# Projections of a hybrid streaming encoder: the low halves of nine weights and nine mixed inputs move from VectorE to GpSimd

## The chip, the cores and the metric

The kernel runs on one core of a Trainium2 chip. The core has five engines with a queue each: TensorE (PE in the profile; its weight loads are PEld), VectorE (DVE), ScalarE (ACT), GpSimd (POOL) and SyncE (SP, which issues the DMAs). Each works through its own instructions in the order in which they were written out when the program was built, and waits on semaphores where an instruction needs the result of another engine. The metric is the device time of one execution, in microseconds (us); lower is better.

## The reference

Two encoder layers on a sequence of 512 frames with 1024 channels. Layer 0 mixes time with RWKV-7, layer 1 with a Conformer convolution; each is followed by cross-attention to 256 memory tokens and a conv-gated MLP. All inputs and weights are float32. What the change touches is the start of the RWKV mixer, cut to its core here:

```python
xx = jnp.pad(h, ((0, 0), (1, 0), (0, 0)))[:, :T] - h
xr, xw, xk, xv, xa, xg = (h + xx * mu[i] for i in range(6))
r = xr @ w_r                       # 512 x 1024 times 1024 x 1024
k = xk @ w_k
v = xv @ w_v
logw = -softplus(-(w0 + tanh(xw @ w1) @ w2)) - 0.5
decay = exp(-exp(logw))
a = sigmoid(a0 + (xa @ a1) @ a2)
kk = normalised per head(k * k_k)
k = k * (1.0 + (a - 1.0) * k_a)
# then the recurrence over the frames
#   S = S * dec + (S @ -kk) (kk * a)^T + v k^T,   y = S r
# per head of 64 channels, group norm, a bonus from r, k, v, a gate, and @ w_o
```

## The kernel before

Activations lie transposed, 128 channels by 512 frames a tile, eight tiles for 1024 channels. A float32 product is made from three products in a faster format (fp32r): every operand is split into a high half, its cast to fp32r, and a low half, the operand minus that cast, and `mm3` adds high*high, high*low and low*high in PSUM (L181 to L183). The function `split` (L175) does the two steps: ScalarE makes the high half (L176), VectorE the low half by a subtraction with two inputs in SBUF (L177). Every large product of the kernel goes through it.

The three projections run in the order `w_k`, `w_r`, `w_v`. For each, `mixes` makes eight mixed inputs: ScalarE scales h (L368), VectorE adds the shifted part (L369), then `split` gives the pair `xh`, `xl` of 128x512. The input `mf` has two buffers. The weight is read in eight column blocks of 128x1024. The first two blocks are fetched together in two halves by `lead`, so that PE can work on them while the mixed inputs still arrive; the other six (j = 2 to 7) are loaded by SP, split by `wsplit` and used one at a time, 24 matmuls each. The halves `wh` and `wl` have two buffers each: a block's cast can start when PE has finished the block before the previous one.

Other work is woven into the projections. After each block of `w_k`, `k_done` turns k into the decayed keys: matmuls for decay and rate (L521, L540, L541), a long chain on ScalarE and VectorE, and a small weight tile `ws` (ACT L533 and L537, DVE L538) whose zero half GpSimd clears (L532). `r_done` has one product on VectorE with PSUM (L578), two in SBUF (L582) and a matmul (L585). Memory keys and values for the later cross-attention fill gaps (L987, L1043, plain float32). In two groups of four head pairs the kernel inverts small triangular matrices: `subst_a` multiplies (L609), masks (L612), transposes (L618) and then solves by 30 pairs of VectorE steps whose operands all lie in SBUF (L630, L632); `subst_b` transposes the result twice (L640, L642), has GpSimd clear a part of `tt` (L647), copies the rest with ScalarE (L648, L649), and multiplies again (L656, L666). Group 0 starts during `w_k` and ends during `w_r`, group 1 starts during `w_r` and ends during `w_v`. Both lie across the stretches in which the inputs of `w_r` and `w_v` are mixed and split.

Which instruction stands where in an engine's queue is decided by the tile framework's scheduler when the program is built, from the order of the code and its own estimate of durations.

Of the kernel before, what the change touches and what calls it, by code (L numbers as in the profile page):

```python
# [11 lines left out]
ALU = mybir.AluOpType  # L12
# [19 lines left out]
FO = [1, 1, 1, 1, 1, 1, 1, 1]  # L32
FP = 1
NRAW = 4
NGRP = [4, 4, 4, 4, 4, 4, 4, 7]
TB = 'h'
TAS = 'hhhhhhhg'
# [73 lines left out]
class Builder:  # L111
# [51 lines left out]
    def wraw(self, src, cols, rows=128):  # L163
        raw = self.t(self.wp, [128, 1024], "raw", bufs=NRAW)
        self.nc.sync.dma_start(raw[:rows, :cols], src)
        return raw

    def wsplit(self, src, cols):
        raw = self.wraw(src, cols)
        h = self.t(self.wp, [128, 1024], "wh", F32R, bufs=2)  # L170
        l = self.t(self.wp, [128, 1024], "wl", F32R, bufs=2)
        self.split(raw[:, :cols], h[:, :cols], l[:, :cols])
        return h, l

    def split(self, src, h, l):  # L175
        self.nc.scalar.copy(h, src)  # L176
        self.nc.vector.tensor_tensor(out=l, in0=src, in1=h, op=ALU.subtract)  # L177

    def mm3(self, out, lh, ll, rh, rl, start, stop):
        mm = self.nc.tensor.matmul  # L180
# [10 lines left out]
    def lead(self, srcs):  # L191
# [3 lines left out]
        for half in range(2):  # L195
            raw = self.t(self.wp, [128, 1024], "raw", bufs=NRAW)
            for j in range(2):
# [4 lines left out]
            ws.append((h, l))  # L202
        return ws

    def gemm_cols(self, srcs, xs, evac, lead=None, between=None):

        ws = lead or self.lead(srcs)
        pss = [self.ps() for _ in range(2)]
        for k, (xh, xl) in enumerate(xs):
            for j in range(2):  # L210
                w = ws[k // 4]
                s = slice(j * 512 + k % 4 * 128, j * 512 + k % 4 * 128 + 128)
                self.mm3(pss[j], w[0][:, s], w[1][:, s], xh, xl, k == 0, k == len(xs) - 1)
        if between:
            between()
        for j in range(len(srcs)):
            if j < 2:
                ps = pss[j]
            else:
                w = self.wsplit(srcs[j], 1024)  # L220
                ps = self.ps()
                self.gemm(ps, w, xs)
            evac(j, ps)
# [100 lines left out]
    def rwkv(self):  # L324
        nc, a = self.nc, self.a
        with ExitStack() as cx:
# [27 lines left out]
            h = self.x  # L354
# [7 lines left out]
            for i in range(KT):  # L362
                nc.vector.scalar_tensor_tensor(out=h[:, i, :], in0=h[:, i, :], scalar=self.vec("g_mix0", i),
                                               in1=rs, op0=ALU.mult, op1=ALU.mult)

            def mix(m, i, tag="mf", bufs=2):
                mf = self.t(self.gp, [128, T], tag, bufs=bufs)
                nc.scalar.activation(mf, h[:, i, :], AF.Copy, scale=cpr[:, (5 + m) * KT + i : (5 + m) * KT + i + 1])  # L368
                nc.vector.scalar_tensor_tensor(out=mf[:, 1:], in0=h[:, i, : T - 1], scalar=self.vec(f"mu{m}", i),  # L369
                                               in1=mf[:, 1:], op0=ALU.mult, op1=ALU.add)  # L370
                return mf
# [19 lines left out]
            for i in range(KT):  # L391
                mf = mix(5, i, "xh", KT)
# [9 lines left out]
            def mixes(m):  # L402
                xs = []
                for i in range(KT):
                    mf = mix(m, i)
                    xt = self.xtile()
                    self.split(mf, *xt)
                    xs.append(xt)
                return xs

# [4 lines left out]

            rslot = lambda: self.t(self.wp, [128, D], "raw", bufs=NRAW)
            for j in range(NU0, NST):
# [34 lines left out]
            for w, m, done in (("w_k", 2, k_done), ("w_r", 0, r_done),  # L452
                               ("w_v", 3, v_done)):
                srcs = [a[w][p] for p in range(NP)]
                lead = self.lead(srcs)
                self.gemm_cols(srcs, mixes(m), done, lead)
            self.gates = [self.t(r1, [128, T], n) for n in ("za", "zl")]
            nc.sync.dma_start(self.gates[0], self.gpark[0:128])
            for r0 in (0, 32, 64):
# [12 lines left out]
            lead = self.lead(wo)  # L472
# [579 lines left out]
    def xattn(self, layer):  # L1052
        nc, a = self.nc, self.a
        kd, vd = self.kvd[0, layer], self.kvd[1, layer]
        with ExitStack() as cx:
# [67 lines left out]
            for n4 in range(2):  # L1123
                raw = self.t(self.wp, [128, 1024], "raw", bufs=NRAW)
                for j in range(2):
# [13 lines left out]
    def ffn(self, layer):  # L1139
        nc, a = self.nc, self.a  # L1140
        with ExitStack() as cx:
# [63 lines left out]
            if layer == 0:  # L1205
# [3 lines left out]
                for u in self.vunits[:NKV]:  # L1209
                    self.lower(NKP, lambda: u(lambda: self.t(self.wp, [128, D], "raw", bufs=NRAW), lambda: self.t(ap, [128, T], "z", bufs=2)))  # L1210
                del self.vunits[:NKV]


    def conv(self):
        nc, a = self.nc, self.a
        PADW = CW - 1
        with ExitStack() as cx:
# [31 lines left out]
            def in_done(j, ps):  # L1249
# [17 lines left out]
                for h in range(2):  # L1267
                    own, oth = slice(64 * h, 64 * h + 64), slice(64 - 64 * h, 128 - 64 * h)
                    for d, s in zip(s_[h], (uh, ul)):
                        nc.scalar.copy(d[own], s[own])  # L1270
                        nc.scalar.copy(d[oth, 0 : W - 1], s[own, 1:W])  # L1271
                ng = NGRP[i]
                pcs = [self.ps(TP), self.ps(TB)]
# [51 lines left out]
            def late_values():  # L1325
                self.vmem[:] = self.memory1(lambda: self.t(up, [128, D], "kvm", bufs=2))
                for u in self.vunits:
                    u(lambda: self.t(self.wp, [128, D], "raw", bufs=NRAW), lambda: self.t(up, [128, T], "vl", bufs=KT))

# [157 lines left out]
```

## Time and profile before

| what | us |
|---|---|
| median of three runs | 1658.86 |
| the three runs | 1658.69, 1660.44, 1658.86 |
| the profiled execution | 1656.06 |
| its span, first to last instruction | 1654.3 |
| PE busy (share of the span) | 1613.1 (98%) |
| DVE busy | 1106.0 (67%) |
| ACT busy | 794.8 (48%) |
| POOL busy | 73.1 (4%) |

All times of the trace are counted from the start of the span of this one execution. A busy PE is not PE at its peak, because the ends of matmuls are modelled; a wait of PE is what counts. The projections run from about 64 us to about 291 us of the span: `w_k` to 141, `w_r` to 238, `w_v` after that.

### The profile page before, as it was taken

The numbers are of one execution on the slowest core, as the hardware profiler recorded it, in microseconds if no ns is written. First come the engines' busy times: TensorE is split into PE (matmuls) and PEld (weight loads), VectorE is DVE, ScalarE is ACT, GpSimd is POOL, SyncE is SP. The second block draws the span as 40 slices with busy tenths as digits, with TensorE's granted clock in tenths as the row PEclk, the third lists the DMA queues.
The fourth block names the chain that finished last, engine by engine and source line by source line (L and its number), as shares of the span: only waits on it lengthen the run. The fifth ranks groups of instructions, "written<-read, shape, count | busy, mean of one in ns | idle before, by whom it ended". The sixth has DMA issues, their size and how long they took to land. (4 is left out here: it accounts for less than half of the span.)

```text
span 1654.3 us, 24232 instructions
## 1 busy us (share of the span) xinstructions
PE 1613.1 (98%) x9742; PEld 1293.5 (78%) x9742; DVE 1106.0 (67%) x1795; ACT 794.8 (48%) x1242; POOL 73.1 (4%) x101
## 2 busy tenths in 40 slices
PE   7999989899999999999999999999999999999998
PEld 6575558898888888888888777767888888888887
DVE  4779976568766667777732479877766677777323
ACT  5876635766454344434422366645533434444222
POOL 0000000000000000000000024430000000000000
PEclk9999999999999999999999999999999999999999
DMA  6333322103441233332333331223412333323332
GB/s 237 114 99 109 105 65 90 53 22 115 135 140 51 86 120 94 98 103 90 96 95 94 112 107 51 65 89 103 140 52 89 91 98 94 102 92 93 97 95 83
DMA packets 55151, 159.77 MB, mean 97 GB/s; under 512 B 6144, under 2 KB 10368, under 8 KB 55040
## 3 DMA queue, kind: packets, MB, share of 16 engines
q1 hardware_dynamic: 55040, 158.24, 30.8%
q8 instruction: 76, 1.25, 0.3%
q14 instruction: 35, 0.29, 0.1%
HBM read 150.55 MB, written 7.67 MB: 96 GB/s over the span
## 5 line engine op out<-in xcount | busy, mean ns | idle before, releaser
L176 ACT CAST wh<-raw 128x1024 fp32r<-128x1024 f32 (+1 forms) x227 | 235.1, 1037 | 503.4 <-PE g L182 396.2
L182 PE MATMUL g<-xl,wh 128*128 128x512 f32 x1152 | 451.0, 392 | 4.1 <-DVE xl L177 3.6
L181 PE MATMUL g<-xh,wh 128*128 128x512 f32 x1152 | 452.9, 394 | 0.7 <-ACT xh L176 0.7
L183 PE MATMUL g<-xh,wl 128*128 128x512 f32 x1152 | 451.0, 391 | 2.5 <-DVE wl L177 2.5
L177 DVE TENSOR_TENSOR wl<-raw,wh 128x1024 fp32r<-128x1024 f32 (+1 forms) x227 | 274.7, 1210 | 164.2 <-ACT wh L176 163.8
L182 PEld LDWEIGHTS g<-xl,wh 128*128 128x128 f32 x1152 | 216.9, 188 | 54.0 <-DVE xl L177 6.6
L183 PEld LDWEIGHTS g<-xh,wl 128*128 128x128 f32 x1152 | 216.9, 188 | 50.4 <-DVE wl L177 3.3
L181 PEld LDWEIGHTS g<-xh,wh 128*128 128x128 f32 x1152 | 216.9, 188 | 48.4 <-issue 1.8
L181 PE MATMUL g<-ah,wh 128*128 128x512 f32 (+1 forms) x374 | 141.0, 377 | 0.0
L183 PE MATMUL g<-ah,wl 128*128 128x512 f32 (+1 forms) x374 | 140.9, 377 | 0.0
L182 PE MATMUL g<-al,wh 128*128 128x512 f32 (+1 forms) x374 | 140.9, 377 | 0.0
L1157 DVE TENSOR_TENSOR z<-g,rs 128x512 f32<-128x512 f32 x88 | 60.4, 688 | 70.8 <-PE g L183 69.2
L181 PEld LDWEIGHTS g<-ah,wh 128*128 128x128 f32 x374 | 70.4, 188 | 13.0
L182 PEld LDWEIGHTS g<-al,wh 128*128 128x128 f32 x374 | 70.4, 188 | 12.9
L183 PEld LDWEIGHTS g<-ah,wl 128*128 128x128 f32 x374 | 70.4, 188 | 12.7
L1277 POOL TENSOR_TENSOR dg<-i,wsp 128x256 fp32r<-128x256 f32 x70 | 48.2, 721 | 657.3 <-DVE wsp L1231 573.0
L176 ACT CAST ah<-tmp 128x512 fp32r<-128x512 f32 x44 | 27.3, 622 | 100.9 <-DVE z L1156 95.8
L1299 DVE SCALAR_TENSOR_TENSOR h<-u,cdw,h 128x512 f32<-128x512 f32 x98 | 73.8, 753 | 2.3
L321 DVE TENSOR_TENSOR x<-x,g 128x512 f32<-128x512 f32 x39 | 26.8, 688 | 68.7 <-PE g L183 68.7
L1162 DVE SCALAR_TENSOR_TENSOR tmp<-z,fdw,tmp 128x512 f32<-128x512 f32 x88 | 66.0, 752 | 2.9
L1161 DVE SCALAR_TENSOR_TENSOR tmp<-z,fdw,tmp 128x512 f32<-128x512 f32 x88 | 65.5, 746 | 0.4 <-ACT tmp L1160 0.4
L1160 ACT ACTIVATE tmp<-z,fdw 128x512 f32<-128x512 f32 x88 | 63.2, 720 | 4.7 <-DVE z L1157 1.5
(351 smaller groups left out, 2445.4 us busy)
## 6 DMA issues: line engine op xcount, KB each, us to landing
raw<-wi SPq DMA_DIRECT2D x84, 512.0 KB, 3.5
raw<-wo SPq DMA_DIRECT2D x33, 512.0 KB, 3.5
raw<-wv SPq DMA_DIRECT2D x16, 512.0 KB, 3.6
raw<-cwi SPq DMA_DIRECT2D x14, 512.0 KB, 3.6
raw<-wq SPq DMA_DIRECT2D x12, 512.0 KB, 4.4
raw<-wxo SPq DMA_DIRECT2D x12, 512.0 KB, 3.5
raw<-wo SPq DMA_DIRECT2D x16, 384.0 KB, 3.1
raw<-wk SPq DMA_DIRECT2D x10, 512.0 KB, 3.8
```

What stands on the lines that cost most here:

```text
L176: self.nc.scalar.copy(h, src)
L177: self.nc.vector.tensor_tensor(out=l, in0=src, in1=h, op=ALU.subtract)
L181: mm(out, lh, rh, start=start, stop=False)
L182: mm(out, lh, rl, start=False, stop=False)
L183: mm(out, ll, rh, start=False, stop=stop)
L321: self.nc.vector.tensor_tensor(out=self.x[:, n, :], in0=self.x[:, n, :], in1=ps, op=ALU.add)
L1157: nc.vector.tensor_tensor(out=z[:, 2:], in0=ps, in1=rs(), op=ALU.mult)
L1160: nc.scalar.activation(y, z[:, 2:], AF.Copy, scale=cw(2))
L1161: nc.vector.scalar_tensor_tensor(out=y, in0=z[:, 1 : T + 1], scalar=cw(1), in1=y, op0=ALU.mult, op1=ALU.add)
L1162: nc.vector.scalar_tensor_tensor(out=y, in0=z[:, 0:T], scalar=cw(0), in1=y, op0=ALU.mult, op1=ALU.add)
L1277: nc.gpsimd.tensor_tensor(out=dg[:, h], in0=i2.unsqueeze(1).unsqueeze(1).to_broadcast([128, 2, 2, 64]), in1=wsp[:, :, i, h, 2 * g : 2 * g ...
L1299: nc.vector.scalar_tensor_tensor(out=ac, in0=u[:, jt : jt + T], scalar=cw(jt), in1=ac if n else ln["c"], op0=ALU.mult, op1=ALU.add if n el ...
```

## The change

`split` and `wsplit` take an engine for the subtraction, `gemm_cols` takes the set of column blocks whose low half goes to GpSimd. The three projections use it for the blocks j = 3, 5 and 7 of each weight and for the mixed inputs i = 2, 4 and 6. That is nine subtractions of 128x1024 and nine of 128x512. The casts stay on ScalarE, and all other products of the kernel keep VectorE.

```diff
+SPW = (3, 5, 7)
+SPX = (2, 4, 6)
...
-    def wsplit(self, src, cols):
+    def wsplit(self, src, cols, eng=None):
         raw = self.wraw(src, cols)
         h = self.t(self.wp, [128, 1024], "wh", F32R, bufs=2)
         l = self.t(self.wp, [128, 1024], "wl", F32R, bufs=2)
-        self.split(raw[:, :cols], h[:, :cols], l[:, :cols])
+        self.split(raw[:, :cols], h[:, :cols], l[:, :cols], eng)
         return h, l
 
-    def split(self, src, h, l):
+    def split(self, src, h, l, eng=None):
         self.nc.scalar.copy(h, src)
-        self.nc.vector.tensor_tensor(out=l, in0=src, in1=h, op=ALU.subtract)
+        (eng or self.nc.vector).tensor_tensor(out=l, in0=src, in1=h, op=ALU.subtract)
...
-    def gemm_cols(self, srcs, xs, evac, lead=None, between=None):
+    def gemm_cols(self, srcs, xs, evac, lead=None, between=None, other=()):
...
-                w = self.wsplit(srcs[j], 1024)
+                w = self.wsplit(srcs[j], 1024, self.nc.gpsimd if j in other else None)
...
-                    self.split(mf, *xt)
+                    self.split(mf, *xt, nc.gpsimd if i in SPX else None)
...
-                self.gemm_cols(srcs, mixes(m), done, lead)
+                self.gemm_cols(srcs, mixes(m), done, lead, other=SPW)
```

The line numbers of the changed kernel are two higher than before from `split` on (L179 there is L177 here). The order of instructions moves at many places, because the scheduler reckons with the new engine. Three of them follow.

GpSimd, from the second half of `w_k` to the end of `w_v`. Before, it only clears tiles there (`tmp` is `ws`):

```order
L532 MEMSET tmp_1268 128x256
L532 MEMSET tmp_1350 128x256
L647 MEMSET tt_85 32x32x32 x2
L492 MEMSET c_434_2641 64x1024
L492 MEMSET c_435_2642 64x1024
```

In the changed kernel the same queue holds the subtractions (`xl_1464` is input 6 of `w_r`; `wl_1675`, `wl_2044` and `wl_2116` are blocks 3, 5 and 7 of `w_r`; the last six belong to `w_v`):

```order
L534 MEMSET tmp_1268 128x256
L179 TENSOR_TENSOR xl_1464<-mf_1460,xh_1463 128x512
L534 MEMSET tmp_1350 128x256
L179 TENSOR_TENSOR wl_1675<-raw_1672,wh_1674 128x1024
L179 TENSOR_TENSOR wl_2044<-raw_2041,wh_2043 128x1024
L649 MEMSET tt_85 32x32x32 x2
L179 TENSOR_TENSOR wl_2116<-raw_2113,wh_2115 128x1024
L179 TENSOR_TENSOR xl_2185<-mf_2181,xh_2184 128x512
L179 TENSOR_TENSOR xl_2199<-mf_2195,xh_2198 128x512
L179 TENSOR_TENSOR xl_2213<-mf_2209,xh_2212 128x512
L179 TENSOR_TENSOR wl_2310<-raw_2307,wh_2309 128x1024
L179 TENSOR_TENSOR wl_2374<-raw_2371,wh_2373 128x1024
```

Subtractions and memsets now stand behind each other, so each waits until the ones ahead of it have their inputs.

PE, in `w_r`, around the decay matmuls of the last key block (`h_258_1355`; `g_323_1678` is block 3 of `w_r`, `g_330_1784` block 4, `wl_322_1675` the low half that moves to GpSimd). Before:

```order
L182 MATMUL g_323_1678<-xl_278_1422,wh_321_1674 128x512
L1043 MATMUL kv_306_1535<-raw_332_1814,tt_16_85 128x512
L181 MATMUL g_330_1784<-xh_277_1421,wh_328_1780 128x512
L182 MATMUL g_330_1784<-xl_278_1422,wh_328_1780 128x512
L1043 MATMUL kv_306_1535<-raw_332_1814,tt_16_85 128x512
L540 MATMUL h_258_1355<-zw_13_82,tmp_257_1350 128x512
```

In the changed kernel:

```order
L184 MATMUL g_323_1678<-xl_278_1422,wh_321_1674 128x512
L185 MATMUL g_323_1678<-xh_277_1421,wl_322_1675 128x512
L183 MATMUL g_323_1678<-xh_280_1428,wh_321_1674 128x512
L184 MATMUL g_323_1678<-xl_281_1429,wh_321_1674 128x512
L185 MATMUL g_323_1678<-xh_280_1428,wl_322_1675 128x512
L183 MATMUL g_323_1678<-xh_283_1435,wh_321_1674 128x512
L184 MATMUL g_323_1678<-xl_284_1436,wh_321_1674 128x512
L185 MATMUL g_323_1678<-xh_283_1435,wl_322_1675 128x512
L183 MATMUL g_323_1678<-xh_286_1442,wh_321_1674 128x512
L542 MATMUL h_258_1355<-zw_13_82,tmp_257_1350 128x512
```

Eight more matmuls of block 3 stand ahead of the decay matmuls; the two matmuls of block 4 and three matmuls of the memory values (L1043) went behind them.

ScalarE, in `w_v`, at the end of the second substitution (`wh_405_2373` is the high half of block 5 of `w_v`, `wh_412_2416` of block 6, `x_4_60` holds v, `tt_16_85` and `c4_409_2405` belong to the substitution). Before:

```order
L176 CAST wh_405_2373<-raw_404_2371 128x1024
L449 COPY x_4_60<-g_399_2313 128x512
L648 COPY tt_16_85<-c4_409_2405 32x32x32
L649 COPY tt_16_85<-c4_409_2405 32x32x32
L648 COPY tt_16_85<-c4_409_2405 32x32x32
L649 COPY tt_16_85<-c4_409_2405 32x32x32
L176 CAST wh_412_2416<-raw_411_2414 128x1024
```

In the changed kernel:

```order
L650 COPY tt_16_85<-c4_409_2405 32x32x32
L178 CAST wh_405_2373<-raw_404_2371 128x1024
L451 COPY x_4_60<-g_399_2313 128x512
L651 COPY tt_16_85<-c4_409_2405 32x32x32
L650 COPY tt_16_85<-c4_409_2405 32x32x32
L651 COPY tt_16_85<-c4_409_2405 32x32x32
L178 CAST wh_412_2416<-raw_411_2414 128x1024
```

The cast of block 5 now stands behind the first of the four copies, which needs VectorE's last transpose (L642).

## Rows read from the trace of the kernel before

**Rows 1.** Busy us of the engines by stretch of the projections (PE, PEld, DVE, ACT, POOL):
```profile
64.00:125.00 61.00, 59.76 (x454) 48.26 (x454) 43.31 (x83) 44.91 (x79) 3.16 (x6) 1.00 0.35 110
125.00:200.00 75.00, 69.63 (x417) 43.29 (x416) 73.38 (x164) 48.42 (x78) 2.83 (x5) 0.95 0.38 117
219.00:272.00 53.00, 48.22 (x199) 35.85 (x200) 49.82 (x98) 21.59 (x31) 0.95 (x1) 1.00 0.21 62
272.00:295.00 23.00, 23.00 (x376) 19.44 (x376) 6.20 (x6) 17.24 (x24) 0.95 (x1) 1.00 0.47 142
```
**Rows 2.** Waits of PE from 64 to 296 us: total, times, longest:
```profile
PE g L182 <- DVE xl L177: 3.6, 3, 2.6
...
PE h L540 <- DVE tmp L538: 0.2, 1, 0.2
```
**Rows 3.** Timeline, block 3 of `w_r`: start, us, instruction [idle before <-releaser]:
```profile
175.49 1.05 ACT L176 CAST wh<-raw 128x1024 fp32r<-128x1024 f32 x1
...
191.51 1.22 DVE L177 TENSOR_TENSOR wl<-raw,wh 128x1024 fp32r<-128x1024 f32 x1
...
192.78 0.79 PE L183 MATMUL g<-xh,wl 128*128 128x512 f32 x1 [2.48 <-DVE wl L177]
193.37 0.63 PE L181 MATMUL g<-xh,wh 128*128 128x512 f32 x1
193.79 0.63 PE L182 MATMUL g<-xl,wh 128*128 128x512 f32 x1
...
197.40 0.39 PE L182 MATMUL g<-xl,wh 128*128 128x512 f32 x1
197.63 0.39 PE L183 MATMUL g<-xh,wl 128*128 128x512 f32 x1
```
**Rows 4.** Timeline, input 2 of `w_v`:
```profile
240.08 0.62 ACT L176 CAST xh<-mf 128x512 fp32r<-128x512 f32 x1
...
245.27 0.68 DVE L177 TENSOR_TENSOR xl<-mf,xh 128x512 fp32r<-128x512 f32 x1
...
246.01 0.50 PE L182 MATMUL g<-xl,wh 128*128 128x512 f32 x1 [2.62 <-DVE xl L177]
```
**Rows 5.** Timeline of DVE ahead of the projections, two alike in each row:
```profile
51.82 1.41 DVE L369 SCALAR_TENSOR_TENSOR mf<-x,vecs,mf 128x511 f32<-128x511 f32 x2
...
54.63 2.36 DVE L177 TENSOR_TENSOR wl<-raw,wh 128x1024 fp32r<-128x1024 f32 x2
56.91 1.29 DVE L177 TENSOR_TENSOR xl<-mf,xh 128x512 fp32r<-128x512 f32 x2
```
**Rows 6.** POOL's groups of instructions over the whole span:
```profile
L1245 POOL TENSOR_TENSOR accd<-y 128x512 f32<-128x512 f32 x1 | 1.3, 1286 | 0.0
```
**Rows 7.** Timeline in the convolution, DVE and POOL reading SBUF at one time:
```profile
1066.05 0.76 DVE L1299 SCALAR_TENSOR_TENSOR h<-u,cdw,shift 128x512 f32<-128x512 f32 x1
...
1066.19 1.77 POOL L1245 TENSOR_TENSOR accd<-accd,y 128x512 f32<-128x512 f32 x1
...
1083.64 1.88 DVE L1299 SCALAR_TENSOR_TENSOR h<-u,cdw,shift 128x512 f32<-128x512 f32 x1
...
1083.68 1.29 POOL L1245 TENSOR_TENSOR accd<-accd,y 128x512 f32<-128x512 f32 x1 [0.87 <-DVE y L1305]
```
**Rows 8.** Timeline of `w_r`: memory values, decay matmuls, first matmul behind the second L609:
```profile
175.52 1.88 PE L1043 MATMUL kv<-raw,tt 128*128 128x512 f32 x4
...
185.77 0.23 DVE L538 TENSOR_TENSOR tmp<-w,tmp 64x128 fp32r<-64x128 f32 x1
...
185.91 0.80 PE L540 MATMUL h<-zw,tmp 128*128 128x512 f32 x1
...
219.04 0.50 PE L181 MATMUL g<-xh,wh 128*128 128x512 f32 x1
```
**Rows 9.** Timeline of `w_v`: end of the second substitution and block 5:
```profile
266.74 1.06 ACT L176 CAST wh<-raw 128x1024 fp32r<-128x1024 f32 x1 [3.91 <-PE g L182]
...
268.74 2.04 DVE L642 STREAM_TRANSPOSE c<-c 128x1024 f32<-128x1024 f32 x1
...
270.82 1.05 ACT L648 COPY tt<-c 32x1024 f32<-32x1024 f32 x1 [2.54 <-DVE c L642]
...
272.66 0.39 PE L183 MATMUL g<-xh,wl 128*128 128x512 f32 x1
```

## Prediction

> **What bounds the kernel now.** I read the busy times by stretch first. In all stretches of the projections PE is close to fully busy, so PE sets the time wherever its operands are there; from 125 to 200 us and from 219 to 272 us VectorE is as full as PE (73.4 of 75, 49.8 of 53), from 64 to 125 and after 272 it has room [rows 1]. Then PE's own waits: nine rows, 12.9 us together from 64 to 296 us, of which only some 6 us wait for a low half [rows 2]. That and what the waits cost in clock is all that can be won. The timelines show why a low half is late. The cast of block 3 of `w_r` ends at 176.5, but its subtraction runs at 191.5, because it stands behind the substitution in VectorE's queue. PE waits 2.48 us for it, and then nine intervals between matmuls are 0.43 us and not 0.23: half the clock, some 1.8 us more [rows 3]. Input 2 of `w_v` is the same: cast done at 240.7, subtraction at 245.3, PE waits 2.62 us, this time with no slow matmuls behind it [rows 4]. Both subtractions are among the eighteen that move. So there is a gain to take, 4.3 us and 2.6 us, if GpSimd makes these halves in time and nothing else gets later.
>
> **What one moved subtraction costs.** On VectorE a pair takes 2.36 and 1.29 us, where one takes 1.23 and 0.69, so in a full queue a weight costs 1.13 and an input 0.60 [rows 5]. On GpSimd the trace has the 128x512 form with two inputs: 1.29 us [rows 6]. The 128x1024 form is not there; twice that is 2.56 (below, 1.29 if all of it were a fixed cost; above, 2 x 1.77 = 3.54 if the stretched row of 128x512 [rows 7] were the rule; I take twice the undisturbed row). The halves come later by 0.6 and 1.4 us than VectorE would make them if it were free, but VectorE is not.
>
> The row that decides is another. At 1083.64 VectorE starts a product with two inputs in SBUF and GpSimd an addition 0.04 us later: VectorE's takes 1.88 us. At 1066.05 the same product starts 0.14 us ahead of GpSimd: it takes 0.76, and GpSimd's addition 1.77 in place of 1.29 [rows 7]. They do not run side by side: one waits for the other. GpSimd's 1.29 us cost VectorE 1.12. So a moved input blocks a full VectorE for 1.12 and a moved weight for about 2.4 (2.56 less the same 0.17), against 0.60 and 1.13 saved: +0.5 and +1.3 us each. In the two full stretches nearly all VectorE work is of that kind: the steps of the substitution (L630, L632), the key products, L369, L582. The bounds of this price are zero, if GpSimd slips into VectorE's idle time, and the full duration.
>
> The Trainium skill says the same in "SBUF — State Buffer", section "Who interferes with whom": VectorE's second read port is GpSimd's, an instruction with two SBUF inputs contends for it, and the loser blocks for the whole instruction. By the page's full blocking the prices are 1.29 and 2.56 and the time is 1.5 us longer than the one forecast; the rows give 1.12, and they are used. The rows agree with the page that this is blocking and not sharing. "GPSIMD Engine Reference", section "Performance versus the Vector engine", has 4497 ns for 2048 columns, from which I estimate 2.25 us for 1024; four such steps are on the path below, so by it the time is 1.2 us shorter.
>
> **The sum, stretch by stretch.**
>
> 64 to 125 us (`w_k`): three inputs, three weights. VectorE is busy 43.3 of 61 us [rows 1] and fits the blocks into its idle time; no wait of PE there is for a low half. Cost 0; without that cover 3 x 0.5 + 3 x 1.3 = 5.4. A library load of GpSimd stands ahead of its first subtraction, where the engine has nothing else to do: 0. A `raw` buffer is given back up to 1.4 us later, but casts wait for PE and not for a DMA (3.91 us, [rows 9]): 0, and up to 1.4 a block without that cover. The memsets L532 now stand behind subtractions whose casts come later; ScalarE's L537 waits for them, then VectorE's L538 and PE's L540, which waits for VectorE anyway (next step): 0.
>
> 125 to 219 us: VectorE loses three inputs and gets three blocks (+1.6), is blocked 2.4 by block 3, which GpSimd now takes as soon as it is cast, and makes one L369 of `w_v` earlier (0.67, half a pair with its overlap [rows 5]): +4.7. Of its 1.6 us of idle time [rows 1] I let 1.0 absorb that: +3.7. So L538 of the last key block, done at 186.0, is done at 189.7, and PE, which started L540 right behind it at 185.91 [rows 8], must wait there: the order puts less work ahead. From there to the first matmul behind the second L609 (219.04) PE takes 33.1 us. The new order puts behind L540 three matmuls L1043 (0.94 each, from a pair of 1.88 [rows 8]) and two of block 4, and ahead of it eight of block 3 at 0.23: 2.8 + 0.5 - 1.8 = +1.5. The wait of 2.48 and the 1.8 of low clock go: -4.3. Sum 3.7 + 1.5 - 4.3 = +0.9: the second substitution starts 0.9 later.
>
> 219 to 271 us: VectorE's queue is one chain from L618 to the end of L642 at 270.8 [rows 9], with the mixing of `w_v` in it. It loses three inputs and two weights (4.1) and is blocked 3 x 1.12 + 2 x 2.4 = 8.2: +4.1, of which I let idle time take 0.5: +3.6. The gain of 2.62 at input 2 does not last: what is late next is input 3, whose L369 stands behind the same blocks on VectorE.
>
> Block 5 of `w_v`: its cast ran at 266.74, before the copies [rows 9]. Now it stands behind the first L648, and that behind L642. Behind the end of L642 come the copy (1.05), the cast (1.06), GpSimd (2.56) and some 0.1 of semaphores: 4.8 us, where before PE's first matmul with this low half came 1.9 us behind (272.66 after 270.78 [rows 9]): +2.9. Behind it the cast of block 6 and its users follow in the same order as before and PE is busy without a gap (23.00 of 23 [rows 1]), so nothing gives the time back.
>
> Together 0.9 + 3.6 + 2.9 = +7.4: the matmul of 272.66 comes at about 280. The profiled execution of 1656.06 becomes 1663.5. The median of the runs shown is 2.8 above that execution, so I forecast **1666.3 us** for the median, 0.45% slower.
>
> **The rivals.**
>
> *Side by side, and faster.* VectorE and GpSimd do not hinder each other here, since the inputs are small and GpSimd finds gaps. Then VectorE gains 0.6 and 1.13 at each step: L540 has no wait: PE comes to it 1.5 earlier, has the 1.5 of reordered work behind it and saves 4.3, -4.3 at 219; then -4.1 on the chain, then still +2.9 at block 5: -5.5, 1653.4 us. PE's waits, 12.9 plus 1.8, leave room for that. For it: both long waits of PE are for moved halves. Against it: the two rows of the convolution. With f for the share of the blocks that VectorE feels, the sum is about 14 f - 6.1 (blocks 5.8 + 8.2; savings 1.8 + 4.1, the two waits 4.3, idle time 1.0, against 0.7, 1.5 and 2.9): under f = 0.43 it turns to faster.
>
> *Half the blocks hide.* GpSimd's reads fall into VectorE's transposes, PSUM products and small steps half of the time. Then the prices about equal the savings: the L369 moved ahead and half of block 3's block less 1.0 of idle give +0.9 at L538, -1.9 at 219, 0 on the chain, +2.9: +1.0, 1659.9 us, no change that can be told.
>
> *New waits lower the clock.* Each of three new waits of 2 us and more (L540, input 3 of `w_v`, block 5) could bring matmuls at 0.43 us behind it as in [rows 3]: +1.8 each, 1668 to 1672 us. Against it: no slow matmul follows the 2.62 us of [rows 4].
>
> **How the numbers follow.** Forecast 0.50 (its own range 1662.5 to 1668), low clock on top 0.11, half 0.18, side by side 0.21. The range takes in all but the outer half of the first rival and the end of the third: 1653.5 to 1670.5. A change of under 0.2% (3.3 us) can't be told from none on this kernel; faster than 1655.5 has 0.21, the middle 0.19, slower than 1662.2 has 0.60.
>
> **What will show it.** Right: in the profile after, POOL has 18 more TENSOR_TENSOR, weights near 2.6 us alone and longer beside VectorE; L630, L632 and L369 show instructions stretched by 1 to 2.4 us; PE's wait for `wl` at 192.8 is gone, PE waits for L538 before the last L540, for `xh` of input 3 of `w_v`, and for a POOL `wl` of block 5 behind L648. Wrong: if L630 and L632 keep their durations the first rival holds; if a POOL weight takes under 2 us the chain loses little; if PE waits in `w_k` for POOL, my zero there is wrong.

## The result

The changed kernel takes 1671.24 us (median of 4 runs, 1670.26 to 1672.79), the kernel before, run beside it, 1658.78 (4 runs). The ratio is 1.0080, 95% interval 1.0067 to 1.0092: slower by 12.5 us, where 7.4 were forecast, and 0.7 us above the range. The profiled execution takes 1670.26 (before 1656.06, and 1663.5 forecast), its span 1668.0 (before 1654.3).

Line numbers of the changed kernel and of the experiments are two higher than before from `split` on: L179 is the subtraction, L542 the decay matmul (before L540), L620 the first transpose of a substitution (L618), L644 the last one (L642), L650 the copy behind it (L648).

The busy times by stretch, with the columns of [rows 1], say first that VectorE did not get emptier in the first of its two full stretches: it lost eighteen subtractions in all, but from 125 to 200 us it is as full as before (73.4 of 75). From 219 to 272 us it is busy for 45.3 us, where it was 49.8.

```profile
125.00:200.00 75.00, 68.02 (x297) 41.89 (x296) 73.42 (x157) 43.07 (x71) 7.87 (x7) 0.98 0.32 103
200.00:219.00 19.00, 17.33 (x410) 9.91 (x409) 14.61 (x20) 10.16 (x16) 4.80 (x3) 1.00 0.35 114
219.00:272.00 53.00, 43.75 (x281) 30.72 (x280) 45.26 (x86) 19.29 (x30) 11.35 (x5) 0.94 0.13 42
```

The groups of GpSimd over the whole span show its side of the price: a moved weight takes 2.51 us on the mean, a moved input 1.61, where the two weights behind 280 us, with VectorE idle, take 2.38 and 2.39, and the shortest input takes 1.27.

```profile
L179 POOL TENSOR_TENSOR wl<-raw,wh 128x1024 fp32r<-128x1024 f32 x9 | 22.6, 2513 | 89.7 <-ACT wh L178 77.6 <-PE kv L989 12.1
L179 POOL TENSOR_TENSOR xl<-mf,xh 128x512 fp32r<-128x512 f32 x9 | 14.5, 1609 | 113.8 <-ACT xh L178 113.8
```

The timeline of the changed kernel around its last key block: two subtractions of GpSimd, and the product of VectorE that began next to each.

```profile
181.81 2.92 POOL L179 TENSOR_TENSOR wl<-raw,wh 128x1024 fp32r<-128x1024 f32 x1 [5.79 <-ACT wh L178]
...
182.50 2.78 DVE L568 SCALAR_TENSOR_TENSOR BK<-AR,vecs,tmp 64x512 f32<-64x512 f32 x1
...
189.65 0.51 PE L542 MATMUL h<-zw,tmp 128*128 128x512 f32 x1 [1.62 <-DVE tmp L540]
...
196.92 0.50 PE L185 MATMUL g<-xh,wl 128*128 128x512 f32 x1 [1.56 <-DVE wl L179]
...
203.33 2.91 POOL L179 TENSOR_TENSOR wl<-raw,wh 128x1024 fp32r<-128x1024 f32 x1 [18.60 <-ACT wh L178]
...
204.01 2.77 DVE L572 SCALAR_TENSOR_TENSOR AR<-AR,cpr 128x504 f32<-128x504 f32 x1
...
219.84 1.21 PE L611 MATMUL kv<-AR,BK 64*32 64x32 f32 x66 [1.67 <-issue]
...
223.54 0.25 PE L611 MATMUL kv<-AR,BK 64*32 64x32 f32 x3 [1.11 <-issue]
...
224.28 2.09 DVE L620 STREAM_TRANSPOSE c<-c 128x1024 f32<-128x1024 f32 x1
```

L568 and L572, each with two inputs in SBUF, take 0.74 alone and 2.78 and 2.77 here, until GpSimd is done. The wait at 189.65 answers to 185.91 in [rows 8], where there was none. The 2.48 us for block 3 [rows 3] is gone, but PE waits 1.56 for block 4, still on VectorE behind the transposes. The second substitution starts with L620, 4.7 us later than its L618 before, shown here with the waits of PE ahead of it:

```profile
217.25 1.08 PE L609 MATMUL kv<-AR,BK 64*32 64x64 f32 x63 [0.43 <-ACT tt L616]
218.90 0.21 PE L609 MATMUL kv<-AR,BK 64*32 64x32 f32 x1 [0.56 <-issue]
...
219.61 2.10 DVE L618 STREAM_TRANSPOSE c<-c 128x1024 f32<-128x1024 f32 x1
```

The end of the second substitution in the changed kernel, against [rows 4, 9]:

```profile
255.16 1.22 PE L183 MATMUL g<-xh,wh 128*128 128x512 f32 x2 [2.30 <-ACT xh L178]
...
269.60 2.48 POOL L179 TENSOR_TENSOR wl<-raw,wh 128x1024 fp32r<-128x1024 f32 x1 [5.74 <-ACT wh L178]
...
269.85 2.32 DVE L634 TENSOR_TENSOR c<-c,c 128x84 f32<-128x84 f32 x1
...
277.54 2.07 DVE L644 STREAM_TRANSPOSE c<-c 128x1024 f32<-128x1024 f32 x1
279.65 1.05 ACT L650 COPY tt<-c 32x1024 f32<-32x1024 f32 x1 [6.59 <-DVE c L644]
280.60 1.04 ACT L178 CAST wh<-raw 128x1024 fp32r<-128x1024 f32 x1
...
281.72 2.38 POOL L179 TENSOR_TENSOR wl<-raw,wh 128x1024 fp32r<-128x1024 f32 x1 [9.65 <-ACT wh L178]
...
284.15 0.50 PE L185 MATMUL g<-xh,wl 128*128 128x512 f32 x1 [0.85 <-POOL wl L179]
```

A small step of the substitution, 0.25 us alone, takes 2.32. Between 125 and 272 us GpSimd makes ten of the eighteen halves, and beside each of them one row of VectorE is stretched, by 0.8 to 2.1 us, 13.6 together: 6.9 ahead of the second L620, 6.7 behind it. The matmul that came at 272.66 comes at 284.15, +11.5.

### The profile page after: what moved, and what is told of

Read it like the earlier page. It is cut to its first block, busy times and chain, and to the rows that moved or that the text cites. A ratio compares the mean times of both kernels' runs of the same rounds, so it can differ in the third digit from the quotient of the medians.

```text
span 1668.0 us, 24233 instructions
## 1 busy us (share of the span) xinstructions
PE 1619.1 (97%) x9742; PEld 1295.2 (78%) x9742; DVE 1108.0 (66%) x1777; ACT 794.9 (48%) x1242; POOL 110.1 (7%) x119
## 5 line engine op out<-in xcount | busy, mean ns | idle before, releaser
L179 DVE TENSOR_TENSOR wl<-raw,wh 128x1024 fp32r<-128x1024 f32 (+1 forms) x218 | 263.7, 1210 | 163.0 <-ACT wh L178 162.3
L1159 DVE TENSOR_TENSOR z<-g,rs 128x512 f32<-128x512 f32 x88 | 60.4, 688 | 71.0 <-PE g L185 69.8
```

The lines of the kernel that those rows point to most:

```text
L179: (eng or self.nc.vector).tensor_tensor(out=l, in0=src, in1=h, op=ALU.subtract)
L1159: nc.vector.tensor_tensor(out=z[:, 2:], in0=ps, in1=rs(), op=ALU.mult)
```

## The experiments

In the edits SPW and SPX are written by weight, and "changed" is `SPW = SPX = all three`; only what differs is shown. Each ratio is to the kernel before, run beside it, with its 95% interval. The marks are read from the timeline of one execution each, in us, from start to start but for the end of L644: **a** from the first L620 to the last pair of L542, **b** from there to the second L620, **c** from there to the end of the second L644, **d** from there to the first matmul L700 of the recurrence. "Stretched" is the sum over the rows of VectorE from 125 to 272 us beside GpSimd, less what the same form takes alone.

| kernel | median us | ratio | a | b | c | d | stretched |
|---|---|---|---|---|---|---|---|
| before | 1658.78 | | 54.5 | 33.7 | 51.2 | 23.4 | 0 |
| changed | 1671.24 | 1.0080 (1.0067 to 1.0092) | 58.2 | 34.6 | 55.3 | 26.2 | 13.6 |
| wk_only | 1657.58 | 0.9999 (0.9989 to 1.0008) | 54.6 | 33.3 | 53.1 | 23.4 | 0 |
| wr_only | 1664.95 | 1.0047 (1.0033 to 1.0061) | 58.2 | 36.1 | 52.4 | 24.4 | |
| wv_only | 1660.92 | 1.0018 (1.0009 to 1.0027) | 54.5 | 32.8 | 54.1 | 23.2 | |
| one_input | 1665.49 | 1.0044 (1.0032 to 1.0057) | 55.0 | 34.2 | 51.3 | 27.2 | 5 |
| write_only | 1658.28 | 0.9999 (0.9990 to 1.0008) | 54.1 | 32.3 | 49.6 | 26.2 | 0.2 |
| no_r5 | 1670.66 | 1.0074 (1.0062 to 1.0087) | 58.2 | 34.8 | 55.5 | 26.2 | |
| no_v5 | 1669.52 | 1.0071 (1.0059 to 1.0084) | 58.5 | 34.7 | 54.1 | 25.1 | |
| full_r4 | 1674.23 | 1.0100 (1.0086 to 1.0114) | 60.4 | 33.0 | 55.8 | 26.3 | |
| r34_only | 1661.26 | 1.0021 (1.0012 to 1.0029) | 58.5 | 31.7 | 52.2 | 23.4 | |
| gate34 | 1656.20 | 0.9992 (0.9984 to 1.0001) | 54.5 | 33.2 | 51.4 | 23.4 | |
| gate3 | 1658.48 | 1.0002 (0.9993 to 1.0011) | 54.5 | 31.4 | 51.4 | 23.4 | |
| few_instr | 1668.80 | 1.0070 (1.0057 to 1.0083) | 58.2 | 33.3 | 55.5 | 24.2 | |

How far marks scatter without a cause in the change can be seen in wk_only: PE and ScalarE have the order of before, and its c is 1.9 longer (below, in the part on the hardware).

**Which projection.**

```diff
-SPW, SPX = all three
+SPW, SPX = w_k alone        (wk_only)
+SPW, SPX = w_r alone        (wr_only)
+SPW, SPX = w_v alone        (wv_only)
```

> Only the three blocks and three inputs of w_k go to GpSimd; PE and ScalarE have the order of the kernel before. Theory: VectorE has idle time there (41.8 of 61 us busy with the change), so blocks of 0.5 to 1.6 us on it disappear: 1658.8, within 1 us of before, and the first matmul of w_r and the last L542 come within 0.5 us of before. Rival (blocked rows in w_k reach the keys and so the substitution): L542 1 to 2 us later, 1660 to 1661.

> Only the three blocks and three inputs of w_r go to GpSimd. Theory (each stretch has its own price, blocking above all): the second L620 comes 4.7 us later than before, as in the changed kernel, block 7 adds 0.5 on the substitution behind it, and the cast of block 5 of w_v stands ahead of L650 as before, so nothing more: 1657.7 + 5.2 = 1662.9. Rival (the price is in w_v, and what w_r loses is given back by the slack before the substitution): L620 within 1 us of before and 1658.5.

> Only the three blocks and three inputs of w_v go to GpSimd; PE and ScalarE have the order of the kernel before up to w_v, and the cast of block 5 stands ahead of the copies L650. Theory: L620 within 0.5 of before; the substitution from L620 to the end of L644 takes 54 to 55 us where it took 51.2 (three inputs and block 3 block VectorE by 5, of which 2.9 are saved subtractions, some idle time goes); block 5 adds at most 1.2: 1657.7 + 3.9 = 1661.6. With wr_only the sum is 9.1, and the other 3 or so of the whole change are the place of the cast of block 5, which only the whole change moves. Rival (the parts only cost together): 1658.5.

As the theory has it for `w_k`: nothing. `w_r` costs 7.8 us by its ratio, 2.6 more than expected, with a as in the changed kernel and b longer still; `w_v` costs 3.0, in c alone, a little less than expected. Together that is 10.8 of 13.3 by the ratios: both parts cost by themselves, and neither rival holds. What is left fits the 2.8 in d, which the whole change has (`w_r` alone has 1.0 of it, the other two none), though the intervals are too wide to prove that.

**Reads or order.** In one kernel GpSimd reads one tile in place of two, in the other (almost) none; the order of all engines stays, in the second up to the inputs of `w_v`.

```diff
-        (eng or self.nc.vector).tensor_tensor(out=l, in0=src, in1=h, op=ALU.subtract)
+        eng.tensor_scalar(out=l, in0=h, scalar1=src[:, 0:1], scalar2=None, op0=ALU.mult) if eng else ...
...
-        (eng or self.nc.vector).tensor_tensor(out=l, in0=src, in1=h, op=ALU.subtract)
+        (eng.tensor_tensor(out=l[:, 0:1], in0=src[:, 0:1], in1=h[:, 0:1], op=ALU.subtract),
+         eng.memset(l.bitcast(F32), 0.0), eng.memset(l.bitcast(F32), 0.0)) if eng else ...
```

> The changed kernel with the same eighteen instructions on GpSimd in the same places, behind the same casts, but each reads one tile of SBUF instead of two (the high half times one column of the source), so the low halves hold other values; every engine has word for word the order of the changed kernel. Theory (two-input reads of VectorE and of GpSimd block each other): if a one-input read doesn't block, no row of VectorE is stretched beside GpSimd (in the changed kernel ten rows between 125 and 272 us are, by 0.8 to 2.1 us each), the last L542 has no wait of 1.6, L644 ends some 10 us earlier than the 279.6 of the changed kernel, and the time is 1658 to 1662. Rival (the new order and the lateness of GpSimd's halves cost the time, not the blocking): 1669 to 1671. Third case (one input blocks as much as two): the same stretched rows and 1671.

> The changed kernel, but on GpSimd each of the eighteen subtractions is a subtraction of one column and two memsets of the whole low half, which read nothing (so the low halves hold zeros and a part of the products is left out); they wait for the same casts. The orders are those of the changed kernel up to the inputs of w_v, where some matmuls change places. one_input still had stretched rows, 4.9 us in all between 125 and 272 us against 13.6 in the changed kernel, and cost 7.3 us against 13. Theory (what is left there is the rest of the blocking plus the new order): with no reads no row of VectorE is stretched, the last L542 comes 54.5 us behind the first L620 as before, the second L620 88.2 to 89.2, and the time is the price of the new order alone, by the line through the two kernels some 4 us: 1661.5, ratio 1.0024 (1.001 to 1.0035). Rival (GpSimd blocks VectorE whenever it is busy, reads or not): stretched rows of 0.3 us and more, 1664 and more.

The same product L568 beside block 3 of `w_r`, in one_input and then in write_only:

```profile
178.85 3.37 POOL L179 TENSOR_SCALAR wl<-wh,raw 128x1024 fp32r<-128x1024 f32 x1 [5.80 <-ACT wh L178]
...
179.53 1.50 DVE L568 SCALAR_TENSOR_TENSOR BK<-AR,vecs,tmp 64x512 f32<-64x512 f32 x1
```
```profile
178.74 0.75 DVE L568 SCALAR_TENSOR_TENSOR BK<-AR,vecs,tmp 64x512 f32<-64x512 f32 x1
178.82 1.97 POOL L179 MEMSET wl<- 128x1024 f32 x2
```

Stretched by 2.04, 0.76 and 0.01: the three kernels differ in what GpSimd reads, and the time goes 1.0080, 1.0044, 0.9999. One_input fell between its theory and its rival because one read blocks too, only less. Write_only did better than its theory: without the blocking, the new order and the work that VectorE is spared come to nothing together. Its marks gain in a, b and c (0.4, 1.4 and 1.6) and give 2.7 back in d. So without the blocking there is no loss. What the order costs by itself no run separates. The straight line from which I had expected 4 us for it was wrong.

**One step back on VectorE.** The orders of PE and ScalarE are those of the changed kernel.

```diff
-SPW["w_r"] = (3, 5, 7)
+SPW["w_r"] = (3, 7)         (no_r5)
...
-SPW["w_v"] = (3, 5, 7)
+SPW["w_v"] = (3, 7)         (no_v5)
```

> The changed kernel, but block 5 of w_r is subtracted on VectorE again; the order of PE and of ScalarE stays word for word that of the changed kernel. Theory (blocking): in the changed kernel the GpSimd subtraction at 203.33 holds the key product L572 for 2.77 us where it takes 0.74, and that is a part of what my sum left out between the last L542 and the second substitution. Without it L572 takes 0.74, the transpose L620 (224.28 in the changed kernel) comes about 2.0 earlier, near 222.3, and the time falls by about 2 us, to 1669.2. Rival (the waits behind the last L542 come from the order and from L542 itself being late): L572 is short but L620 stays within 0.5 of 224.3 and the time stays at 1671.

> The changed kernel, but block 5 of w_v is subtracted on VectorE again; the order of PE and of ScalarE stays that of the changed kernel, with the cast behind the first L650. It splits the term of 2.9 us that I gave to block 5. Theory (the term is mostly the place of the cast): the cast still waits for the end of L644; VectorE makes the half in 1.22 where GpSimd takes 2.38, so only PE's wait of 0.85 us for it goes, and the matmul that comes 4.5 us behind the end of L644 comes 3.7 behind: 1670.4 us. Rival (the term is GpSimd's slowness): the whole 2.7 us goes, the matmul comes about 1.9 behind the end of L644, and the time is 1668.5.

In no_r5 the product L572 is short again, and L620 is no earlier: the rival holds. What decides there is not the block but when PE gets through the matmuls L611.

```profile
204.51 0.74 DVE L572 SCALAR_TENSOR_TENSOR AR<-AR,cpr 128x504 f32<-128x504 f32 x1
...
220.40 1.21 PE L611 MATMUL kv<-AR,BK 64*32 64x32 f32 x66 [2.53 <-issue]
...
224.91 1.99 DVE L620 STREAM_TRANSPOSE c<-c 128x1024 f32<-128x1024 f32 x1
```

In no_v5 the first matmul with the low half of block 5 comes 3.56 us behind the end of L644 (281.53 and 277.97), where the changed kernel has 4.53 and before 1.88: of the 2.65 lost there 1.0 is GpSimd's slowness and 1.7 the place of the cast behind L650. That is the theory in the trace; as a time no_v5 can't be told from the changed kernel.

**Behind the last L542.**

```diff
-SPW["w_r"] = (3, 5, 7)
+SPW["w_r"] = (3, 4, 5, 7)   (full_r4)
...
-SPW, SPX = all three
+SPW = {"w_r": (3, 4)}; SPX = {}   (r34_only)
```

> The changed kernel, and block 4 of w_r too goes to GpSimd; some matmuls behind the last L542 change places. Theory (the wait of 2.48 us for block 3, which I took for gone, went over to block 4, whose subtraction stands behind the transposes L642 and L644 on VectorE: 1.56 us at 196.92): GpSimd makes this half beside the transposes, which read one tile and aren't blocked, the wait goes, and L620 comes 1.5 earlier than the 224.3 of the changed kernel: 1669.7. Rival (whatever is made early there is lost again at the next wait of PE, L587 or L611): L620 within 0.5 of 224.3, 1671.

> Of all the eighteen only blocks 3 and 4 of w_r go to GpSimd, the two on which PE waits around the transposes L642 and L644 (2.48 us before, 1.56 us in the changed kernel). Theory: the block of 2.0 us by block 3 falls on the keys ahead of the last L542, which comes 1.5 late; the wait of 2.48 goes and no other half stands behind the transposes, so L620 comes 1 to 2.5 earlier than before: 1655.5 to 1657, the one part of the change that could pay. Rival (the waits pass on to L587 and L611): L620 as before or up to 1 later, 1657.5 to 1659.

In time both theories missed: expected were 1669.7 (full_r4) and at most 1657 (r34_only), measured 1674.23 and 1661.26. In the marks they are right behind the last L542 and wrong ahead of it. Behind it the wait for block 4 is gone, and b falls by 1.6 (full_r4) and to 31.7 (r34_only); how much of that comes from L542 itself being late, these two can't tell. Ahead of it the subtraction of block 4 falls on one more product of VectorE, not on the transposes, and L542 comes 2.2 us (full_r4) and 4.0 us (r34_only) later. In r34_only the two blocks and their effect stand alone:

```profile
176.58 2.38 POOL L179 TENSOR_TENSOR wl<-raw,wh 128x1024 fp32r<-128x1024 f32 x1 [21.16 <-ACT wh L178]
...
176.66 2.42 DVE L632 TENSOR_TENSOR c<-c,c 128x108 f32<-128x108 f32 x1
...
184.76 2.37 POOL L179 TENSOR_TENSOR wl<-raw,wh 128x1024 fp32r<-128x1024 f32 x1 [5.55 <-ACT wh L178]
184.77 2.90 DVE L572 SCALAR_TENSOR_TENSOR AR<-AR,cpr 128x504 f32<-128x504 f32 x1
...
189.91 0.50 PE L542 MATMUL h<-zw,tmp 128*128 128x512 f32 x1 [3.83 <-DVE tmp L540]
```

2.15 and 2.16 us of stretch, 4.0 us of delay. So the next two kernels hold the subtractions back until VectorE has gone on to the transposes:

```diff
     def split(self, src, h, l, eng=None):
         self.nc.scalar.copy(h, src)
+        eng and self.gate is not None and eng.tensor_tensor(out=l[0:64, 0:1], in0=self.gate, in1=self.gate, op=ALU.add)
...
-        pw, pa = pl
+        pw, pa = pl; self.gate = ws[0:64, 1, 0:1] if p == 7 else None
...
+SPW = {"w_r": (3, 4)}; SPX = {}   (gate34)
+SPW = {"w_r": (3,)}; SPX = {}     (gate3)
```

> The kernel before with blocks 3 and 4 of w_r on GpSimd, and each of the two subtractions held back by a GpSimd instruction of 64 elements that reads the last product L540 of the keys: so GpSimd starts when VectorE goes on to the two transposes, L642 and L644, which read one tile each and were not stretched beside GpSimd in wv_only. PE keeps the order of before up to the last L542. Theory (what blocked the keys in r34_only was the time at which GpSimd worked, not the work): the last L542 comes as early as before (54.5 us behind the first L620, where r34_only had 58.5), no row of VectorE is stretched by more than 0.5 ahead of it, block 3's half is there about 3 us earlier than before, and from the last L542 to the second L620 it takes 31.7 us as in r34_only, where before took 33.7: 2 us faster, 1656.2, ratio 0.9988. Rival (the gain behind L542 came only from L542 being late, so that VectorE had done more ahead of it): from L542 to L620 33 us and more, 1658.

> As gate34, but block 4 stays on VectorE, behind the transposes. Theory: the wait of PE goes over from block 3 to block 4 or goes, since VectorE now makes block 4's half where it made block 3's (1.2 us earlier): from the last L542 to the second L620 about 32 to 33 us, between before and gate34: 1657, ratio 0.9993. Rival: as before, 1658.

```profile
186.13 2.12 DVE L642 STREAM_TRANSPOSE c<-c 128x1024 f32<-128x1024 f32 x1
...
186.67 4.71 POOL L179 TENSOR_TENSOR wl<-raw,wh 128x1024 fp32r<-128x1024 f32 x2
...
188.15 1.94 DVE L644 STREAM_TRANSPOSE c<-c 128x1024 f32<-128x1024 f32 x1
...
189.12 0.50 PE L185 MATMUL g<-xh,wl 128*128 128x512 f32 x1 [1.50 <-POOL wl L179]
...
189.94 2.52 DVE L551 TENSOR_TENSOR_SCAN tmp<-cst,tmp 128x512 f32<-128x512 f32 x1
```

In gate34's timeline (above) the transposes take 2.12 and 1.94 beside GpSimd, about as alone (2.04 in [rows 9]), L542 is in time, and block 3's matmul comes at 189.1 where it came at 192.8 [rows 3]. The place was the fault, as expected. But b is 33.2, the rival's sign, and not 31.7: block 4 still falls on the scan L551 (2.52 us, 1.2 alone), and thirteen matmuls of the weight blocks run at half the granted clock there, where before had ten. Gate3 has the same wait of 1.5 us for block 3, no such stretch of low clock, and a b of 31.4. These are the rows of before, gate34 and gate3, with the columns of [rows 1]:

```profile
190.50:197.00 6.50, 4.22 (x10) 3.35 (x11) 6.34 (x11) 6.36 (x9) 0.00 (x0) 0.50 0.63 194
```
```profile
191.00:197.50 6.50, 6.50 (x61) 5.28 (x56) 6.36 (x11) 6.30 (x9) 2.27 (x3) 0.50 0.76 235
```
```profile
185.60:217.00 31.40, 27.15 (x575) 17.79 (x574) 25.64 (x38) 18.29 (x29) 4.46 (x4) 1.00 0.35 109
```

So a difference of 2 us in b between two single traces can be the clock and not the edit. The gain of gate34, 0.08% or 1.3 us, can't be told from none, and gate3 shows none: neither kernel beats the one before by more than the runs can tell.

```diff
-            ps = self.ps("kv")
-            for j in range(16):
+            ps = self.ps("kv") if half == 0 or grp else ps
+            for j in range(16 if half == 0 or grp else 0):
```

> The changed kernel with the second halves of the matmuls L658 and L668 of the first group left out (64 and 64 records of 32x32; the copies behind them take the first half's result instead), so part of the inverse is not computed. It asks what PE's waits inside L611 are that the profile puts down to issue (1.67 and 1.11 us in the changed kernel, 0.56 before). In all ten kernels so far PE goes on 1.25 to 1.48 us after a 16 KB packet of the instruction queue has landed. Theory (PE has used up its instructions, because in the changed order the small matmuls L658, L668 and L611 stand closer together): with 128 small matmuls fewer the next packet is asked for later and PE finds more ahead of it: the issue waits inside L611 together fall below 1 us, and from the last L542 to the second L620 (34.6 us) it takes 2.4 us of matmuls and some 2 us of waits less: about 30.5. Rival (the waits belong to L611 itself, whatever stands ahead): they stay at 2 us and more, about 32.2 us.

The edit stands in both loops, L658 and L668. The theory fails: the issue waits in L611 are 1.91 and 0.81, together 2.7 us as in the changed kernel, which is the rival's sign (2 us and more), though b is 33.3 and neither number. But a packet of the instruction queue still lands ahead of each end of a wait. With 128 small matmuls fewer there is one packet less and the next lies elsewhere, and PE waits in the same place. What the waits are is read from the records alone (in the part on the hardware); what sets their length stays open.

## Why the prediction was wrong

The direction and the main mechanism held: the blocking was forecast from two rows of the convolution [rows 7], and write_only shows that without it the change costs nothing. The path behind the last L542 was wrong. By terms:

- `w_k`, forecast 0: held (wk_only).
- L538 of the last key block, +3.7: measured +3.74 (L542 at 189.65, before 185.91). That it fits so well is in part luck: four blocked rows ahead of it make 4.9 us where 5.8 were reckoned, and less idle time took it up than the 1.0 assumed.
- **The step that failed** stands behind it: "The wait of 2.48 and the 1.8 of low clock go: -4.3", by which the second substitution starts 0.9 later. It starts 4.7 later. The wait and the slow matmuls did go (the granted clock is 1.00 from L542 to L620, where before had 0.50 from 190.5 to 197 us), but I did not ask what is late next. Block 4, which stays on VectorE behind the same transposes, waits 1.56; and PE's waits inside L611, 0.99 together before (0.43 and 0.56), are 3.32 (0.25, 1.67, 0.29, 1.11). That is 3.9, about the missing 3.8. For the first there is full_r4, where the wait is gone and b falls by 1.6, but there L542 is late as well; the second is only read from the trace, and its cause stays open.
- The chain to the end of L642, +3.6: measured +4.2, close to it by luck. Blocked were 6.7 us, not 8.2, and the 4.1 of moved subtractions can't all have been saved. If the 1.6 that write_only gains in c stands for the saving, these two give +5.1; no run shows what took up the rest. In write_only VectorE waits 2.0 us for ScalarE in that stretch (before 0.3), so its time is not all worth saving. The wait for input 3 of `w_v` came as forecast (2.30 at 255.16).
- Block 5 of `w_v`, +2.9: measured +2.65, for the reason given (no_v5).

Together that is +11.5 at the matmul of 284.15. The other 2.2 us of the profiled span lie behind it. From the first L700 to the end it takes 1362.2 us and before 1360.1; wk_only, with the order of before, takes 1361.7, so most of that is what executions differ by.

The first rival (side by side) is out as a case, and out as a gain too: write_only nearly fulfils its condition, where it forecast -5.5, and the kernels are the same. Half the blocks hiding is out: in the two full stretches none of the ten did. New waits lowering the clock happened in part. The granted clock is 0.50 right behind a wait of 2.39 us for L587 at 234.36 and behind the 2.30 for input 3, and 1.00 behind the waits for L542 and for block 5:

```profile
235.00:238.00 3.00, 3.00 (x7) 1.76 (x6) 2.73 (x9) 0.00 (x0) 0.00 (x0) 0.50 0.20 81
255.20:258.50 3.30, 3.28 (x7) 2.17 (x8) 3.23 (x7) 2.00 (x4) 1.59 (x1) 0.50 0.10 38
```

Counted to 300 us, these two and one near 144 us are the changed kernel's stretches of low clock; sixteen matmuls start in them, where ten start in the one of before. What the difference is worth no run tells. In both rows VectorE is busy nearly all the time (2.73 of 3.00 and 3.23 of 3.30 us), so it need not be PE that sets the pace there. The measured 1671.24 lies in this rival's 1668 to 1672, but the marks put most of the excess into the failed step.

## What to carry to other kernels

In this kernel GpSimd left a full VectorE alone only where it did not read SBUF beside VectorE's two-input products: when it only wrote (but for the small copies named below), or when VectorE transposed or read PSUM. Before moving a step, list what VectorE runs at the moment the moved step becomes ready, not only how full it is. When a wait is counted as won, name the next operand behind the same cause: here block 4 stood behind the same two transposes as block 3. A step that becomes ready earlier on an idle engine starts earlier, and may hit the worst moment; holding it back by a dependency (gate34) kept the path free, though it won no time that the runs can tell.

## What the hardware showed

**Blocking in detail.** With two inputs on both sides each engine holds the other, whichever is first: VectorE's rows are stretched by 0.8 to 2.1 us, and GpSimd's subtraction of an input takes up to 3.01 us (1.27 alone) when VectorE steps follow each other. Not stretched were STREAM_TRANSPOSE (2.12 and 1.94 beside GpSimd) and the product L580 with one input in PSUM (0.68, of which 0.65 lie beside GpSimd). The Trainium skill says in "SBUF — State Buffer", section "Who interferes with whom", that an instruction of VectorE with two SBUF inputs contends with a GpSimd instruction that reads SBUF and not with one that only writes it: write_only agrees, with no two-input row of VectorE stretched by the memsets. Its rule that the one that comes second blocks for the whole instruction, which stands there for VectorE's two-port modes and which the prediction took for all, differs from one_input, where a GpSimd instruction of 2.85 us alone stretched L568 by 0.76.

Memsets are not free of it altogether: in the kernel before, a copy of 128x8 on VectorE, 0.17 us in other blocks, takes 0.92 beside a memset of GpSimd that only writes, and in write_only such a copy takes 0.54 and a product of 128x8 with one input (L574) 0.42 in place of 0.23.

```profile
94.28 1.94 POOL L647 MEMSET tt<- 32x1024 f32 x2 [12.98 <-PE kv L987]
...
95.34 0.92 DVE L553 COPY G<-AR 128x8 f32<-128x8 f32 x1
```

**Waits of PE behind the instruction queue.** In fourteen traces PE has 21 waits inside L611 that the profile puts down to issue, each ending 1.19 to 1.48 us after a packet of 16 KB of the instruction queue has landed. In the changed kernel the DMA view of 217.4 to 218.4 us has one such packet (5.8% of sixteen engines' 1.0 us, so 0.93 us, 217.46 to 218.39) ahead of the matmul at 219.84, that of 221.0 to 222.2 another (1.02 us, landed at 222.09) ahead of the one at 223.54; the columns are packets, MB and share:

```profile
q8 instruction: 1, 0.02, 5.8%
```
```profile
q8 instruction: 1, 0.02, 5.3%
```

The Trainium skill, "Runtime: NRT & Kernel Launch", section "Instruction fetch mechanics", calls crossing such a block mostly hidden; in these stretches, where a matmul starts every 15 ns or so (66 from 219.84 to 220.83), PE waited 0.3 to 3.3 us. That the packet ends the wait fits all 21, but no run has taken the packet away alone.

**The clock from execution to execution.** wk_only has PE's order of before and the same wait of 2.61 at input 2 of `w_v` [rows 4], but behind it, from 248.0 to 253.3 us, the granted clock is 0.51, the lower of its two levels (1.2 of 2.4 GHz), where the trace of before has 1.00. The row of wk_only, then that of before, with the columns of [rows 1] (the clock is the third number from the end):

```profile
248.00:253.30 5.30, 5.30 (x13) 4.16 (x14) 4.69 (x10) 3.25 (x5) 0.00 (x0) 0.51 0.17 15
```
```profile
248.00:253.30 5.30, 4.56 (x19) 3.18 (x18) 5.30 (x11) 3.63 (x6) 0.00 (x0) 1.00 0.08 9
```

PE makes 13 matmuls there and not 19, the casts behind them come later, c is 1.9 longer, and still the medians are the same: a single trace can hold or miss such a stretch, and the marks of two traces can differ by some 2 us through it.
